# A convolution moved wholly to VectorE, a fused masked copy in a matrix inverse, and another instruction scheduler, in a two-block kernel

## The chip, the cores and the metric

The kernel runs on one core of a Trainium2 chip. The metric is the time of one execution in microseconds (us) on the device. Before the change three runs took 1193.18, 1193.24 and 1193.87 us, with a median of 1193.24 us.

The core has five engines with a queue each: TensorE (PE, with its weight loads PEld), VectorE (DVE), ScalarE (ACT), GpSimd (POOL) and SyncE (SP), which here issues the loads and stores. Each engine works through its own instructions in the order that was fixed when the kernel was built, and waits on semaphores for the others.

## What is computed

Two transformer blocks on 512 tokens of width 1024, in fp32. Cut to what matters here:

```python
# block 1: grouped attention (8 query heads, 2 key heads, 256 context keys) beside a conformer convolution
u = rms_norm(h, norm_w) * (1 + scale) + shift        # shift, scale, gate from c @ w_mod
p = u @ w_in                                         # q, k, v, gates za, glu a|g, gates zc
u2 = a * sigmoid(g)                                  # 512 tokens x 512 channels
y = depthwise_conv(u2, conv_w) + conv_b              # width 31, centred
conv = (silu(layer_norm(y)) @ w_pw + b_pw) * silu(zc)
h = h + gate * (concat(attention * silu(za), conv) @ w_out)

# block 2: rwkv7 time mix (12 heads of 64, delta rule) beside attention to 256 memory tokens, then a feed-forward
slab = token_shift((rms_norm(h) @ rw_in), mu)        # r, k, v, decay, rates, gate
for t in range(512):                                 # per head, state S is 64 x 64
    S = S * w_t + (S @ a_t) b_t^T + v_t k_t^T
    y_t = S @ r_t
x = x + concat(mix, memory_attention) @ w_out
x = x + square(relu(rms_norm(x) @ w_ff1)) @ w_ff2
```

## The kernel before

Features lie on the 128 partitions and tokens along the free axis, so a tile is mostly 128x512. Every fp32 product of the large projections is made of three matmuls (`mm3`, line 181): weights and activations are split into a high and a low part (`wh`, `wl` and a pair of `hg`, `U` or `A` tiles), and hi·hi, hi·lo and lo·hi are added in PSUM. A projection (`proj`, line 189) of one 128-column slab is 8 such triples, 24 matmuls. The high part of a weight is an ACT copy, the low part a DVE subtraction (`wl<-wr,wh`); SP loads the raw weights (`wr`) two at a time, so a load waits until the DVE subtraction has released a buffer.

**Block 1** (`block1`, line 345). The start loads `w_mod` (24 loads of 512 KB, ten buffers `modw`) and `w_start` (8 loads, two buffers `wr`), makes shift, scale and gate, normalises x to the pairs `U`, and accumulates six projections at once. `glu` turns three pairs of them into the convolution's inputs `up[0..2]` (tiles `hg`); a fourth comes after the projections `pa` and `pg`. Then follow q (four token groups in the PSUM tiles `s`), the context norm (tiles `tA`, `modw`), k and v (six token tiles), eight gate projections (`zgate`, each 24 matmuls, a tanh on ACT and one DVE operation `hg<-tA,pj`), rope and the head norms (tiles `xb`, `kn`, `nr`), the first two heads' queries (`xa<-pt,xa` on DVE), their scores (`s<-kst,xa`), and the attention, with the convolution's layer norm and pointwise product put between its heads.

The convolution has 4 channel tiles of 31 taps. The middle tap with the bias is an ACT operation that initialises `y`; the 30 others (120 in all) are spread over three engines by hand-written tables. Tiles 0 and 1 (60 taps): ACT multiplies into a tile `cv` and POOL adds (`conv_pool`; `tick` releases one tap per so many matmuls, `PACE`). Tile 2 and half of tile 3 (45 taps): one DVE `scalar_tensor_tensor` each (`conv_vec`, counts `CVQ` and `CVZ`), written into the program between the q groups and after each gate. The other 15 taps of tile 3: two POOL operations each (`conv_self`).

**Block 2** (`block2`, line 1292). Six pairs of heads. Each pair has three projections (r, k, v), a preparation (`prep`), and two groups of four 128x128 units. `gen_abc` (line 945) inverts each group's triangular matrices in 16 steps: matmuls into the PSUM tile `i`, evictions on ACT and DVE into the f16 tiles `f`. Early in it DVE makes three masked tiles `Dm`, `DT` and `P1`; then three more masked copies of `Lh`, called `OT`, are made by three POOL multiplications of 128x512, and later `IX` (identity minus X) by one more. `gen_chain` (line 1104) carries the state over the chunks (`sb`, `st`, `y`). The steps of all generators are merged by a table of due times, with the projections cut into eight pieces each (`PIECES`), and the program is written in that order. After the last pair the feed-forward runs over `w_ff1` and `w_ff2` until the end.

The build's scheduler takes the program as written and orders each engine's queue; its default is used before the change.

Of the kernel before, what the change touches and what calls it, by code (L numbers as in the profile page):

```python
# [13 lines left out]
F16 = mybir.dt.float16  # L14
# [11 lines left out]
KT = 8  # L26
# [309 lines left out]
PACE = 6  # L336
CVZ = (2, 1, 2, 0, 3, 4, 3, 3)
CVQ = (8, 9, 9, 8)
CTX = (0, 2)
CONV = (0, 0, 0, 0, 0, 0, 0, 0)  # L340
CSELF = (30, 0, 0, 1, 0, 1, 0, 0)
# [3 lines left out]
def block1(k, I, st, h1d):  # L345
# [130 lines left out]
    todo = [[w for w in range(31) if w != 15] for _ in range(4)]  # L476

    def tap(i):
        w = todo[i].pop(0)
        o0, o1 = max(0, 15 - w), min(S, S + 15 - w)  # L480
        return o0, o1, up[i][:, o0 + w - 15:o1 + w - 15], k.cw[:, i * 31 + w:i * 31 + w + 1]

    def conv_init(i):
        y = ys[i] = k.t("hg")
        A.activation(y, up[i], AF.Identity, scale=k.cw[:, i * 31 + 15:i * 31 + 16], bias=k.vec("conv_b", i))

    def conv_pool():
        r = yield
        for i in (0, 1):
            conv_init(i)  # L490
            while todo[i]:
                o0, o1, u, w = tap(i)
                p = k.t("cv")
# [8 lines left out]
    cp = conv_pool()
    pace = [0]

    def tick(r, n=1):
        pace[0] += n
        while pace[0] >= PACE:
            pace[0] -= PACE
            cp.send(r)

    def conv_self(i, n):
        if ys[i] is None:
            y = ys[i] = k.t("hg")
            G.tensor_scalar(out=y, in0=up[i], scalar1=k.cw[:, i * 31 + 15:i * 31 + 16], scalar2=k.vec("conv_b", i), op0=ALU.mult, op1=ALU.add)
        for _ in range(min(n, len(todo[i]))):
            o0, o1, u, w = tap(i)
            p = k.t("cv")
            G.tensor_scalar(out=p[:, o0:o1], in0=u, scalar1=w, scalar2=None, op0=ALU.mult)
            G.tensor_tensor(out=ys[i][:, o0:o1], in0=ys[i][:, o0:o1], in1=p[:, o0:o1], op=ALU.add)

    def conv_vec(i, n):
        if ys[i] is None:
            conv_init(i)
        for _ in range(min(n, len(todo[i]))):
            o0, o1, u, w = tap(i)
            V.scalar_tensor_tensor(out=ys[i][:, o0:o1], in0=u, scalar=w, in1=ys[i][:, o0:o1], op0=ALU.mult, op1=ALU.add)

    def conv_drain():
        while todo[0] or todo[1]:
            cp.send(None)  # L530
        conv_vec(3, 31)
        assert not any(todo)
# [10 lines left out]
    next(cp)  # L543
    pa, pg = k.t("pj"), k.t("pv")
    proj(k, pa, W1.next(), us, tick=tick)
    proj(k, pg, W1.next(), us, tick=tick)
    glu(pa, pg)

    q_ps = [k.t("s", [2, S]), k.t("s", [2, S])]
    for g in range(4):  # L550
        wh, wl = W1.next()
        for kk in range(2):
            j = 2 * g + kk
            c = slice(kk * S, (kk + 1) * S)
            for t in range(4):
# [5 lines left out]
                tick(T.matmul(ps, ul[:, tt], wh[:, c], start=False, stop=j == KT - 1), 3)  # L561
        conv_vec(2, CVQ[g])
# [15 lines left out]
    for t in (2, 3, 4, 5, 0, 1):  # L578
        ps = k.t("pt", [256])
        for j in range(KT):  # L580
# [7 lines left out]
            tick(T.matmul(ps, ul[:, tt], wh[:, c], start=False, stop=j == KT - 1), 1.5)  # L588
# [1035 lines left out]
```

## Time and profile before

| | |
|---|---|
| median of three runs | 1193.24 us |
| the profiled execution | 1195.04 us |
| its span, first to last instruction | 1193.2 us |
| TensorE busy | 1096.6 us (92%) |
| VectorE busy | 750.1 us (63%) |
| ScalarE busy | 573.7 us (48%) |
| GpSimd busy | 266.3 us (22%) |
| granted TensorE clock, mean | 0.967 |
| chain that ended last, by engine | PE 72%, DVE 17%, ACT 5%, POOL 3% |

The span has four stretches: the start to about 75 us, the rest of block 1 to about 390 us, the time mix of block 2 to about 850 us, and the feed-forward to the end. The matmuls of this core are pipelined, so busy times of TensorE overlap and a busy TensorE is not one at its peak. The granted clock is the share of full TensorE speed that the chip allowed in a stretch; its two levels are 1.2 and 2.4 GHz.

### The profile page before, as it was taken

The numbers are of one execution on the slowest core, as the hardware profiler recorded it, in microseconds if no ns is written. First come the engines' busy times: TensorE is split into PE (matmuls) and PEld (weight loads), VectorE is DVE, ScalarE is ACT, GpSimd is POOL, SyncE is SP. The second block draws the span as 40 slices with busy tenths as digits, with TensorE's granted clock in tenths as the row PEclk, the third lists the DMA queues.
The fourth block names the chain that finished last, engine by engine and source line by source line (L and its number), as shares of the span: only waits on it lengthen the run. The fifth ranks groups of instructions, "written<-read, shape, count | busy, mean of one in ns | idle before, by whom it ended". The sixth has DMA issues, their size and how long they took to land.

```text
span 1193.2 us, 16090 instructions
## 1 busy us (share of the span) xinstructions
PE 1096.6 (92%) x6268; PEld 842.1 (71%) x6268; DVE 750.1 (63%) x1161; ACT 573.7 (48%) x1047; POOL 266.3 (22%) x360
## 2 busy tenths in 40 slices
PE   7997776799999888999999988999999999999998
PEld 3665664565677766666667766776888888888887
DVE  3348999756545469888887688856544334334332
ACT  4346456567843436545464566556534224223220
POOL 0018558780000223334242234100000000000000
PEclk7999887899999989999999999999999999999999
DMA  8752111100123411101011211221232323232332
GB/s 289 251 199 71 36 46 61 53 19 7 48 84 137 123 52 36 37 19 37 19 36 37 62 50 62 72 71 54 88 106 89 105 90 104 90 102 93 99 113 88
DMA packets 30604, 96.47 MB, mean 81 GB/s; under 512 B 3392, under 2 KB 4160, under 8 KB 30528
## 3 DMA queue, kind: packets, MB, share of 16 engines
q1 hardware_dynamic: 30528, 95.45, 24.4%
q8 instruction: 49, 0.80, 0.3%
q14 instruction: 27, 0.22, 0.1%
HBM read 91.24 MB, written 4.19 MB: 80 GB/s over the span
## 4 chain that ended last, share of the span: by engine, by line
PE 72%; DVE 17%; ACT 5%; POOL 3%; issue 2%; DMA 1%; SPq 0%; DVEq 0%; ACTq 0%; POOLq 0%
PE pf L57 29%; PE pj L57 19%; PE i L57 6%; PE pt L57 6%; PE s L57 5%; DVE f L57 5%; PE pv L57 4%; DVE hg L57 3%; PE y L57 2%; POOL nr L57 2%; DVE wl L57 2%; DVE tA L57 1%; DVE p L57 1%; ACT p L57 1%; DVE nr L57 1%
## 5 line engine op out<-in xcount | busy, mean ns | idle before, releaser
L57 ACT ACTIVATE wh<-wr 128x1024 fp32r<-128x1024 f32 (+1 forms) x132 | 137.4, 1042 | 155.0 <-PE pf L57 76.4
L57 DVE TENSOR_TENSOR wl<-wr,wh 128x1024 fp32r<-128x1024 f32 (+1 forms) x132 | 162.3, 1230 | 20.6 <-PE pt L57 7.6
L57 PE MATMUL pj<-hg,wh 128*128 128x512 f32 x448 | 156.3, 417 | 3.2 <-ACT r L57 1.8
L57 PE MATMUL pf<-A,wh 128*128 128x512 f32 x512 | 157.8, 389 | 0.0
L57 POOL TENSOR_TENSOR hg<-hg,cv 128x497 f32<-128x497 f32 (+14 forms) x75 | 112.7, 1503 | 124.3 <-ACT cv L57 116.7
L57 ACT ACTIVATE f<-i 128x512 f16<-128x512 f32 (+1 forms) x132 | 73.2, 598 | 105.1 <-PE i L57 104.9
L57 PEld LDWEIGHTS pf<-A,wh 128*128 128x128 f32 x512 | 95.9, 188 | 19.9
L57 PE MATMUL pf<-A,wl 128*128 128x512 f32 x256 | 99.6, 389 | 0.0
L57 PEld LDWEIGHTS pj<-hg,wh 128*128 128x128 f32 x448 | 81.5, 192 | 19.9 <-ACT r L57 2.0
L57 DVE TENSOR_TENSOR x<-x,pf 128x512 f32<-128x512 f32 (+1 forms) x33 | 22.1, 671 | 113.9 <-PE pf L57 113.9
L57 PE MATMUL i<-f 128*128 128x128 f16 x816 | 69.7, 224 | 24.0 <-DVE f L57 23.6
L57 PE MATMUL pj<-hg,wl 128*128 128x512 f32 x224 | 90.0, 402 | 1.5 <-DVE wl L57 1.5
L57 PEld LDWEIGHTS <-f 128*128 128x128 f16 x864 | 56.7, 100 | 48.5 <-DVE f L57 24.9
L57 PE MATMUL pf<-ff,wh 128*128 128x512 f32 (+1 forms) x272 | 79.7, 377 | 0.0
L57 PE MATMUL pf<-hg,wh 128*128 128x512 f32 x256 | 78.8, 389 | 0.0
L57 DVE SCALAR_TENSOR_TENSOR fr<-pf,r 128x512 f32<-128x512 f32 x32 | 22.1, 691 | 85.4 <-PE pf L57 82.1
L57 ACT ACTIVATE fr<-fr 128x512 f32<-128x512 f32 x32 | 20.2, 632 | 100.2 <-DVE fr L57 100.2
L57 POOL TENSOR_TENSOR f<-f,c 128x512 f16<-128x512 f16 x36 | 48.0, 1361 | 74.1 <-ACT f L57 74.1
L57 PE MATMUL pj<-U,wh 128*128 128x512 f32 x160 | 53.6, 408 | 10.7 <-DVE hg L57 10.7
L57 POOL TENSOR_SCALAR nr<-nr 128x8 f32<-128x8 f32 (+2 forms) x70 | 24.9, 355 | 171.2 <-DVE nr L57 129.1
L57 PEld LDWEIGHTS pf<-ff,wh 128*128 128x128 f32 x272 | 50.1, 188 | 9.5
L57 PEld LDWEIGHTS pf<-hg,wh 128*128 128x128 f32 x256 | 48.0, 188 | 10.0
(303 smaller groups left out, 2368.0 us busy)
## 6 DMA issues: line engine op xcount, KB each, us to landing
wr<-w_ff SPq DMA_DIRECT2D x64, 512.0 KB, 3.5
modw<-w_mod SPq DMA_DIRECT2D x24, 512.0 KB, 7.2
wr<-rw_in SPq DMA_DIRECT2D x20, 512.0 KB, 3.5
wr<-w_out SPq DMA_DIRECT2D x16, 512.0 KB, 3.5
wr<-w_in SPq DMA_DIRECT2D x10, 512.0 KB, 3.5
wr<-w_start SPq DMA_DIRECT2D x8, 384.0 KB, 3.7
x<-xT SPq DMA_DIRECT2D x8, 256.0 KB, 5.7
wr<-w_q SPq DMA_DIRECT2D x4, 512.0 KB, 3.7
```

Of the source, the lines that this page charges most:

```text
L57: r = f(*a, **kw)
```

## The change

There are four parts.

- **The convolution.** All 120 taps become DVE operations. The ACT initialisation and the 30 taps of a tile are written together, the taps inside a block that lowers their scheduling priority by `LATER` = 1500. Tiles 0 to 2 are written before `pa` and `pg`, tile 3 after the fourth `glu`. The tile `cv`, the tables, and the pacing are gone.
- **The inverse.** The three POOL multiplications that made `OT` become one DVE multiplication of 128x1536 f16 (tile `lv`, two buffers; Lh broadcast over three masks). `IX` moves from POOL to DVE. `f` goes from 18 to 12 buffers.
- **The scheduler.** The build is told to order the instructions with `schedule_with_timeline_sim=True`.
- **What follows for the queues.** The new scheduler moves rows on every engine, SP's queue included. At the start SP now issues rows, constants and the rope table amid the `w_mod` loads (before: behind all of them), and the last four `w_start` loads, with the two context loads among them, after the 24th `w_mod` load (before: alternating with groups of four). POOL keeps memsets, casts and the small `nr` chains.

```diff
 LN_AFTER = (4, 4.5, 5, 5.5, 6.5, 7, 7.5, 7.5, 7.5, 8)
 MODW = 10
-PACE = 6
-CVZ = (2, 1, 2, 0, 3, 4, 3, 3)
-CVQ = (8, 9, 9, 8)
+LATER = 1500
 CTX = (0, 2)
-CONV = (0, 0, 0, 0, 0, 0, 0, 0)
-CSELF = (30, 0, 0, 1, 0, 1, 0, 0)
...
-    def conv_pool():
...
-                t = A.activation(p[:, o0:o1], u, AF.Copy, scale=w)
...
-                G.tensor_tensor(out=ys[i][:, o0:o1], in0=ys[i][:, o0:o1], in1=p[:, o0:o1], op=ALU.add)
...
+    def conv(i):
+        u, cw = up[i], lambda w: k.cw[:, i * 31 + w:i * 31 + w + 1]
         y = ys[i] = k.t("hg")
+        A.activation(y, u, AF.Identity, scale=cw(15), bias=k.vec("conv_b", i))
+        with k.tc.high_priority(offset=-LATER):
+            for w in range(31):
+                if w != 15:
+                    o0, o1 = max(0, 15 - w), min(S, S + 15 - w)
+                    V.scalar_tensor_tensor(out=y[:, o0:o1], in0=u[:, o0 + w - 15:o1 + w - 15], scalar=cw(w), in1=y[:, o0:o1],
+                                           op0=ALU.mult, op1=ALU.add)
...
-    next(cp)
+    for i in range(3):
+        conv(i)
     pa, pg = k.t("pj"), k.t("pv")
-    proj(k, pa, W1.next(), us, tick=tick)
-    proj(k, pg, W1.next(), us, tick=tick)
+    proj(k, pa, W1.next(), us)
+    proj(k, pg, W1.next(), us)
     glu(pa, pg)
+    conv(3)
...
-    OT = []
-    for j in range(1, 4):
-        o = k.t("f", [4, P], F16)
-        G.tensor_tensor(out=o, in0=Lh, in1=mk(j), op=ALU.mult)
-        OT.append(o)
+    OT = k.t("lv", [3, 4, P], F16)
+    V.tensor_tensor(out=OT, in0=Lh.rearrange("p (o u) x -> p o u x", o=1).to_broadcast([P, 3, 4, P]),
+                    in1=k.m16[:, 1:4].rearrange("p (j o) x -> p j o x", o=1).to_broadcast([P, 3, 4, P]), op=ALU.mult)
...
-    G.tensor_tensor(out=IX, in0=k.id16x4, in1=X, op=ALU.subtract)
+    V.tensor_tensor(out=IX, in0=k.id16x4, in1=X, op=ALU.subtract)
...
-    k.open(P2, "p2b", dict(lw=1, wa=1, r1=1, AR=2, BK=2, vs=2, UX=2, MT=1, E=3, R4=2, Vs=2, UV=3, W=2, QG=2, sb=2, st=2, f=18))
+    k.open(P2, "p2b", dict(lw=1, wa=1, r1=1, AR=2, BK=2, vs=2, UX=2, MT=1, E=3, R4=2, Vs=2, UV=3, W=2, QG=2, sb=2, st=2, f=12, lv=2))
...
-    with tile.TileContext(nc) as tc:
+    with tile.TileContext(nc, schedule_with_timeline_sim=True) as tc:
```

Three places in the engines' orders, first before and then after the change.

**VectorE, up to the first heads' queries** (`xa<-pt,xa`); `wl` is the low part of a gate's weight, `hg<-tA,pj` a gate's last operation, `kst` the assembled keys. Before:

```order
L57 TENSOR_TENSOR c1_83<-nr_1522,nr_1523 128x44
L57 TENSOR_SCALAR c1_83<-c1_83 128x32 x2
L57 TENSOR_TENSOR wl_1738<-wr_1736,wh_1737 128x1024
L57 TENSOR_TENSOR kst_1603<-pt_1612,kst_1603 64x256
L57 TENSOR_TENSOR kst_1603<-pt_1605,kst_1603 64x512
L57 SCALAR_TENSOR_TENSOR hg_1693<-tA_1691,pj_1648 128x512
L57 TENSOR_TENSOR kst_1604<-pt_1617,kst_1604 64x512
L57 TENSOR_TENSOR kst_1604<-pt_1624,kst_1604 64x256
L57 TENSOR_TENSOR xa_1636<-pt_1630,xa_1635 128x512
L57 TENSOR_TENSOR xa_1645<-pt_1639,xa_1644 128x512
L57 TENSOR_REDUCE c1_83<-s_1699 128x1
```

After:

```order
L57 TENSOR_SCALAR c1_83<-c1_83 128x32 x2
L57 TENSOR_TENSOR wl_1707<-wr_1705,wh_1706 128x1024
L57 SCALAR_TENSOR_TENSOR hg_1666<-tA_1664,pj_1633 128x512
L57 TENSOR_TENSOR kst_1517<-pt_1526,kst_1517 64x256
L57 TENSOR_TENSOR kst_1517<-pt_1519,kst_1517 64x512
L57 TENSOR_TENSOR kst_1518<-pt_1531,kst_1518 64x512
L57 TENSOR_TENSOR kst_1518<-pt_1538,kst_1518 64x256
L57 TENSOR_TENSOR wl_2444<-wr_2442,wh_2443 128x1024
L57 SCALAR_TENSOR_TENSOR hg_1737<-tA_1735,pj_1704 128x512
L57 TENSOR_TENSOR xa_1550<-pt_1544,xa_1549 128x512
L57 TENSOR_TENSOR xa_1559<-pt_1553,xa_1558 128x512
```

Before, six of the eight gates' last operations stand ahead of the first `xa`, and the seventh and eighth behind it. After, all eight stand ahead of it, as do all 120 taps.

**VectorE, the start of one inverse** (third pair, first group): the four `f` rows are the difference L, then `Dm`, `DT` and `P1`; the last `f` row is the eviction of the next product. Before:

```order
L57 TENSOR_TENSOR f_4764<-i_4758,f_4763 128x512
L57 TENSOR_TENSOR f_4767<-UX_4722,c2_3149 128x512
L57 TENSOR_TENSOR f_4768<-f_4763,c2_3149 128x512
L57 TENSOR_TENSOR f_4771<-f_4767,c2_3149 128x512
L57 SCALAR_TENSOR_TENSOR rk_4778<-z_4776,g_58,rk_4778 128x511
L57 TENSOR_TENSOR wl_4783<-wr_4781,wh_4782 128x1024
L57 TENSOR_TENSOR f_4796<-i_4791,c2_3149 128x512
```

After:

```order
L57 TENSOR_TENSOR f_4598<-i_4592,f_4597 128x512
L57 TENSOR_TENSOR f_4601<-UX_4556,c2_2999 128x512
L57 TENSOR_TENSOR f_4602<-f_4597,c2_2999 128x512
L57 TENSOR_TENSOR lv_4666<-f_4597,c2_2999 128x1536
L57 TENSOR_SCALAR st_4576<-y_4568,s8_3570 128x128
L57 TENSOR_TENSOR x_3825<-x_3825,bon_3325 128x512
L57 TENSOR_TENSOR f_4605<-f_4601,c2_2999 128x512
L57 TENSOR_TENSOR f_4630<-i_4625,c2_2999 128x512
```

The new `lv` row stands between `DT` and `P1`, with two operations of other work behind it; the projections' rows `rk` and `wl` that stood behind `P1` are gone from this place.

**TensorE, projections beside the inverse in block 2**; `pj<-hg,wh` and `pj<-hg,wl` are a projection's matmuls, `i<-f` the inverse's, `s` and `y` those of the scores and the state. Before:

```order
L57 MATMUL pj<-p,g 128x512
L57 MATMUL y<-g,sb 128x128
L57 MATMUL s<-AR,BK 128x128 x8
L57 MATMUL pj<-hg,wh 128x512 x2
L57 MATMUL pj<-hg,wl 128x512
L57 MATMUL pj<-hg,wh 128x512 x2
L57 MATMUL pj<-hg,wl 128x512
L57 MATMUL y<-E,UV 64x128 x2
L57 MATMUL y<-QG,st 128x128
L57 LDWEIGHTS f
L57 MATMUL i<-f 128x128
L57 LDWEIGHTS f
```

After:

```order
L57 MATMUL i_3471<-f_3438,lv_3401 128x128
L57 MATMUL pj_3751<-hg_2693,wh_3558 128x512
L57 MATMUL pj_3751<-hg_2694,wh_3558 128x512
L57 MATMUL pj_3751<-hg_2693,wl_3559 128x512
L57 MATMUL pj_3751<-hg_2734,wh_3558 128x512
L57 MATMUL pj_3751<-hg_2735,wh_3558 128x512
L57 MATMUL pj_3751<-hg_2734,wl_3559 128x512
L57 MATMUL pj_3751<-hg_2776,wh_3558 128x512
L57 MATMUL pj_3751<-hg_2777,wh_3558 128x512
L57 MATMUL pj_3751<-hg_2776,wl_3559 128x512
```

Before, the projections stand in pieces of 1 to 10 matmuls between steps of the inverse and the chain. After, many stand in one run: that of `pj_3751`, whose first nine rows are shown, has all its 24 matmuls together. In return several groups of the inverse (about five of the twelve) have no projection between their steps.

## Rows read from the trace of the kernel before

**Rows 1.** The page's part 1: busy us of each engine, share of the span, instructions.

```profile
PE 1096.6 (92%) x6268; PEld 842.1 (71%) x6268; DVE 750.1 (63%) x1161; ACT 573.7 (48%) x1047; POOL 266.3 (22%) x360
```

**Rows 2.** The windows: busy us (count) of each engine by stretch, granted clock, DMA.

```profile
core 0: us, PE busy (x) PEld busy (x) DVE busy (x) ACT busy (x) POOL busy (x), PEclk, DMA share, GB/s
75.00:225.00 150.00, 110.17 (x501) 88.55 (x500) 134.26 (x182) 87.71 (x154) 97.05 (x64) 0.84 0.19 58
180.00:210.00 30.00, 17.52 (x62) 13.49 (x61) 29.71 (x41) 19.87 (x34) 25.90 (x17) 0.78 0.18 53
225.00:245.00 20.00, 17.91 (x88) 14.14 (x88) 14.72 (x24) 11.55 (x22) 19.77 (x14) 1.00 0.08 27
450.00:700.00 250.00, 231.70 (x1905) 174.53 (x1906) 210.59 (x365) 137.27 (x317) 83.24 (x147) 0.99 0.11 35
850.00:1193.00 343.00, 339.61 (x1521) 281.98 (x1519) 135.53 (x158) 101.73 (x125) 0.00 (x0) 1.00 0.30 97
```

**Rows 3.** TensorE's waits from 105 to 245 us: us in total, times, longest.

```profile
PE pj L57 <- DVE tA L57: 10.7, 1, 10.7
PE pj L57 <- DVE hg L57: 10.7, 3, 9.8
```

**Rows 4.** The timeline from 111 to 125 us: start us, us, engine, operation.

```profile
114.12 6.48 POOL L57 TENSOR_TENSOR hg<-hg,cv 128x510 f32<-128x510 f32 x4 [1.02 <-ACT cv L57]
117.76 1.73 DVE L57 SCALAR_TENSOR_TENSOR hg<-hg,c 128x506 f32<-128x506 f32 x1
119.41 1.47 DVE L57 TENSOR_TENSOR tA<-tA 128x256 f32<-128x256 f32 x1
120.81 0.73 DVE L57 SCALAR_TENSOR_TENSOR hg<-hg,c 128x507 f32<-128x507 f32 x1
121.46 0.41 DVE L57 TENSOR_TENSOR tA<-tA 128x256 f32<-128x256 f32 x1
```

**Rows 5.** The chain of waits from 482 to 645 us: its shares by engine and tile.

```profile
by line: PE pj L57 21.8%; DVE f L57 20.1%; PE i L57 17.9%; PE y L57 9.3%; PE s L57 4.0%; DVE p L57 3.7%; POOL nr L57 3.4%; ACT f L57 2.9%; DVE BK L57 2.9%; DVE wl L57 2.5%; issue 2.2%; DVE UV L57 1.8%; DVE z L57 1.7%; DVE rk L57 1.2%; DVE s
```

**Rows 6.** The timeline from 536 to 550 us: one group's inverse begins.

```profile
536.21 4.03 POOL L57 TENSOR_TENSOR f<-f,c 128x512 f16<-128x512 f16 x3 [2.95 <-ACT f L57]
537.52 0.62 PE L57 MATMUL pj<-hg,wh 128*128 128x512 f32 x2
537.85 2.67 DVE L57 TENSOR_TENSOR f<-f,c 128x512 f16<-128x512 f16 x2
537.99 0.40 PE L57 MATMUL pj<-hg,wl 128*128 128x512 f32 x1
539.28 0.62 PE L57 MATMUL i<-f 128*128 128x128 f16 x8 [0.54 <-DVE f L57]
```

**Rows 7.** The timeline at 740 us: `DT` and `P1` of a late group.

```profile
740.45 0.76 DVE L57 TENSOR_TENSOR f<-f,c 128x512 f16<-128x512 f16 x2
```

**Rows 8.** Groups by line, whole span: count, busy us, mean ns, idle before, releaser.

```profile
L57 POOL TENSOR_TENSOR hg<-hg,cv 128x497 f32<-128x497 f32 (+14 forms) x75 | 112.7, 1503 | 124.3 <-ACT cv L57 116.7 <-DVE c L57 3.9
L57 ACT ACTIVATE cv<-hg,c 128x497 f32<-128x497 f32 (+14 forms) x60 | 41.8, 710 | 14.4 <-POOL hg L57 14.2
```

**Rows 9.** The same view: VectorE from 77 to 245 us.

```profile
L57 DVE SCALAR_TENSOR_TENSOR hg<-hg,c 128x497 f32<-128x497 f32 (+14 forms) x45 | 50.3, 1118 | 1.3 <-ACT hg L57 1.1
L57 DVE TENSOR_TENSOR wl<-wr,wh 128x1024 fp32r<-128x1024 f32 x17 | 24.4, 1435 | 7.0 <-PE pv L57 4.2 <-PE pj L57 1.6 <-PE pt L57 1.1
L57 DVE TENSOR_TENSOR tA<-tA 128x256 f32<-128x256 f32 x7 | 6.1, 871 | 0.0
```

**Rows 10.** The same view: VectorE from 450 to 700 us.

```profile
L57 DVE TENSOR_TENSOR f<-i,c 128x512 f16<-128x512 f32 x27 | 18.3, 679 | 1.7 <-PE i L57 1.6
L57 DVE TENSOR_TENSOR wl<-wr,wh 128x1024 fp32r<-128x1024 f32 x15 | 18.2, 1214 | 0.5 <-PE pj L57 0.4
```

**Rows 11.** What SyncE's DMA queue waits for from 0 to 80 us.

```profile
SPq L57 <- DVE wl L57: 42.0, 8, 8.5
```

**Rows 12.** The page's part 6: DMA issues, KB each, median us from issue to landing.

```profile
wr<-w_start SPq DMA_DIRECT2D x8, 384.0 KB, 3.7
```

More of the change, by code (lines that the diff above doesn't have):

```diff
@@ L474, in block1 @@
     ys = [None] * 4
[L476 to L483, printed above, removed]
-        y = ys[i] = k.t("hg")
-        A.activation(y, up[i], AF.Identity, scale=k.cw[:, i * 31 + 15:i * 31 + 16], bias=k.vec("conv_b", i))
-    def conv_pool():
[L488 to L493, printed above, removed]
-                t = A.activation(p[:, o0:o1], u, AF.Copy, scale=w)
-                if r is not None:
-                    k.after(t, r)
-                G.tensor_tensor(out=ys[i][:, o0:o1], in0=ys[i][:, o0:o1], in1=p[:, o0:o1], op=ALU.add)
-                r = yield
-        while True:
-            yield
@@ L502, in block1 @@
[L502 to L532, printed above, removed]
+    def conv(i):
+        u, cw = up[i], lambda w: k.cw[:, i * 31 + w:i * 31 + w + 1]
+        y = ys[i] = k.t("hg")
+        A.activation(y, u, AF.Identity, scale=cw(15), bias=k.vec("conv_b", i))
[5 more added lines that the diff above has]
+                                           op0=ALU.mult, op1=ALU.add)
@@ L560, in block1 @@
                 T.matmul(ps, uh[:, tt], wl[:, c], start=False, stop=False)
-                tick(T.matmul(ps, ul[:, tt], wh[:, c], start=False, stop=j == KT - 1), 3)
-        conv_vec(2, CVQ[g])
+                T.matmul(ps, ul[:, tt], wh[:, c], start=False, stop=j == KT - 1)
         if g == CTX[0]:
@@ L587, in block1 @@
             T.matmul(ps, uh[:, tt], wl[:, c], start=False, stop=False)
-            tick(T.matmul(ps, ul[:, tt], wh[:, c], start=False, stop=j == KT - 1), 1.5)
+            T.matmul(ps, ul[:, tt], wh[:, c], start=False, stop=j == KT - 1)
         kv = k.t("kvs", [256])
@@ L596, in zgate @@
         ps = k.t(tag)
-        proj(k, ps, W1.next(), us, tick=tick)
+        proj(k, ps, W1.next(), us)
         t = k.t("tA")
@@ L664, in zgates @@
             gz.append(zgate(zt[i] if i < 4 else "pj"))
-            conv_vec(3, CVZ[i])
     for i in range(4):
@@ L812, in block1 @@
             zgates(ZG[3 + i])
-            if i == int(LN_AFTER[0]):
-                conv_drain()
             for _ in range(LN_AFTER.count(i)):
                 next(ln, None)
-            conv_vec(3, CONV[i])
-            conv_self(3, CSELF[i])
             if half == 1 and pr < 3:
@@ L1047, in gen_abc @@
         ps = k.t("i")
-        units(ps, OT[j], X, True, True)
+        units(ps, OT[:, j], X, True, True)
         Y = k.t("f", [4, P], F16)
@@ L1506, in emit @@
         p1 = ExitStack()
-        k.open(p1, "p1", dict(c1=1, U=16, tA=4, kvs=6, cv=2))
+        k.open(p1, "p1", dict(c1=1, U=16, tA=4, kvs=6))
         k.open(p1, "p1m", dict(pj=1), PSUM)
```

## The prediction

> **What bounds the kernel now.** I read the page first, then the windows, the waits of TensorE, and last the timelines of the two places that the change touches. TensorE is busy for 92% of the span [rows 1], but evenly so only at the end: in the feed-forward from 850 us it is busy for 339.6 of 343 us with GpSimd at 0 [rows 2]. That stretch is bound by TensorE, holds no edited instruction, and I cost it at 0.
>
> From 75 to 225 us the bound is VectorE. TensorE is busy for 110.2 of 150 us at a granted clock of 0.84, VectorE for 134.3, and in 180 to 210 us VectorE for 29.7 of 30 while TensorE has 17.5 [rows 2]. TensorE's long waits from 105 to 245 us end on VectorE: 10.7 us once for the context norm's `tA`, 10.7 us in three for `hg` [rows 3]. What VectorE does there is slowed by GpSimd: while GpSimd adds its taps from 114.12 to 120.60, a VectorE tap takes 1.73 us and a 128x256 product 1.47; in the next rows, beside no GpSimd operation, they take 0.73 and 0.41, and the product starts 0.65 us after the tap [rows 4]. So a tap in a row of operations costs 0.65 us alone.
>
> In 450 to 700 us VectorE is busy for 210.6 of 250 us, TensorE for 231.7 at clock 0.99 [rows 2]. The chain there alternates: `PE pj` 21.8%, `DVE f` 20.1%, `PE i` 17.9% [rows 5]. The timeline of one group shows the same slowing: GpSimd makes the three `OT` in 4.03 us, and in that time VectorE's `DT` and `P1` take 2.67 us for two, where a late group without GpSimd needs 0.76 [rows 7]; TensorE waits 0.54 us for `DT` [rows 6].
>
> **The change, part by part.** *The convolution, 75 to 245 us.* Removed: 75 GpSimd additions of 1503 ns and 60 ScalarE products of 710 ns [rows 8]; neither engine is full there, so their own time is worth nothing. Added: 75 taps on VectorE, 75 x 0.65 = 49 us. Gained back: VectorE without GpSimd beside it. The 45 taps that it has now take 1118 ns on average, against 0.73: 17.4 us. The 17 `wl` take 1435 against 1214 [rows 9, 10]: 3.8 us. The 7 products `tA` take 871 against 410 [rows 4, 9]: 3.2 us. That is 24 us from three groups. Some forty smaller groups of the same view, each against the shortest duration of its own shape, give an estimated 26 more, so 50 in all. VectorE's work stays as it is, to within 1 us. But the two gates that now stand ahead of the first `xa` move two `wl` and two `hg` there, 2 x (1.21 + 0.68) = 3.8 us (0.68 as for 512 columns from PSUM [rows 10]). VectorE is idle for 15.7 of the 150 us [rows 2]; taps of tiles 0 to 2 need only the start's sums, so they can fill most of it. I take two thirds, 10.5. The first `xa` then comes 10.5 - 3.8 = 7 us earlier. Bounds: all idle time filled gives 12 us earlier; only the three groups' relief gives 26 - 7 = 19 us later.
>
> Behind the first `xa`, in 225 to 245 us, TensorE is busy for 17.9 of 20 us [rows 2], and two of the eight gates stand there now. One gate is 24 matmuls; from the start of two at 537.52 to the third at 537.99 an interval is 0.235 us [rows 6], so a gate is 5.6 us and two are 11. The scores that remain have their own chain with ScalarE and VectorE, so I count 8 of the 11; bounds 0 and 11. Sum for this stretch: -15 us, from +19 to -23. The attention behind it loses GpSimd's and ScalarE's last taps, which hide behind TensorE: 0.
>
> *The start.* SP's queue waits 42.0 us, in 8 times, for VectorE's `wl` to free a `wr` buffer; the longest wait is 8.5 us [rows 11]. In the new order no `w_mod` load stands behind the last four `w_start` loads, so these waits no longer hold `w_mod` back; those four loads in turn stand behind all 24 `w_mod` and the two context loads. A `w_start` load lands 3.7 us after its issue [rows 12]; two pairs that are issued only when they are needed cost 7 us. The longest wait won back is 8 us. I take -2, since the loads alternate less but the buffers are the same: from -8 to +7.
>
> *The inverse, 12 groups.* `DT` and `P1` take 2.67 us for two beside GpSimd [rows 6] and 0.76 in a late group without it [rows 7]. So `DT`, on the chain, ends 0.95 us earlier; 11 groups had it contended, 10 us. `P1` and `IX` follow in 0.41 us or less each, off the chain as long as no eviction waits behind them. GpSimd's `nr` chains no longer queue behind its taps and copies, which I count as nothing gained. The new `lv` is three times as long as an `f<-f,c`: at the f16 rate 0.41 + 2 x 0.27 = 0.95 us, at fp32 rates (1214 ns for 1024, 679 for 512 [rows 10], so 0.535 per 512) 1.75. I take 0.95, for `f<-f,c` is its nearest kin [rows 7] and 0.27 is half of 0.535. It fills the gap from `DT`'s end to the next eviction on VectorE, in which TensorE and ScalarE make the next products. So it costs nothing while that gap is over 0.95 + 0.41 us; without any gap it costs 12 x 1.36 = 16 us, and 26 at the slow price. The Trainium skill (VectorE: DVE Perf Modes, "The perf-mode tier table") gives a product of two 16-bit SBUF tensors two elements a cycle, and its mode needs a step of one in each; the broadcasts here keep that step in the innermost dimension, so by the page the estimate is 0.96 us. No row of this trace shows a broadcast f16 operand.
>
> The same order moves projections into runs of 24. A run is 5.6 us in which a finished eviction has to wait for TensorE. The 18 projections of heads are 101 us of TensorE, and `PE pj` holds 21.8% of the chain already [rows 5], so part of the cost of a run is paid now. I charge 2 us net: -10 + 2 = -8 for block 2, from -23 (the two copies' whole 1.91 us, 12 times) to +37 (below). With `f` at 12 instead of 18 buffers, `OT` has its own two, so no new wait for a buffer is counted.
>
> Sum against the profiled execution of 1195.0 us: -15 - 2 - 8 = -25, or 1170. The runs' median lies 1.8 us lower, so **1168 us**.
>
> **The rivals.** *Projections in clumps* (slower). In three pairs, 163 us, the chain holds 35.5 us of `PE pj` [rows 5], while nine projections need 9 x 5.6 = 50.8: at least 30% hide now between steps that wait for VectorE. If runs of 24 put all into the chain, 18 projections lose 30 us. About five groups have then no filler at all; where TensorE idled, in 180 to 210 us, the granted clock was 0.78 against 0.99 in the busy block 2 [rows 2]. At 0.78 the inverse's 4.9 us of matmul per group (17.9% of 163 us over six groups) grow by 1.3, 7 us for five groups. If lv takes the slow price off the gap, 10 more. Together -10 + 30 + 7 + 10 = +37, and with the -17 of start and block 1 the profiled time is 1215. It decides from +17 on, where 27 of these 47 us are lost. I price it midway between 1195 and 1215: 1205, or 1203 for the runs. For it: `PE pj` leads the chain. Against it: TensorE's waits for `f` are short now, so runs stand where the inverse is waiting anyway. The Trainium skill's Perfetto Trace Analysis, "Matmul Optimizations", wants matmuls in back-to-back batches since the engine's power follows its use; by that rule the runs keep the clock up, and the bare groups let it fall.
>
> *VectorE overfull.* The taps aren't really last: if they stand ahead of `wl`, norm and rope, each is 0.65 us of delay for TensorE. With only the three groups' relief, block 1 is +19 - 8 = +11, and with -2 - 8 it is 1196, or 1194 for the runs: no change. The Trainium skill's Perfetto Trace Analysis, "Optimizing Scalar/DVE Operations", advises moving work off a saturated VectorE to ScalarE or GpSimd, and warns that the two share a read port; by the advice alone the change adds its 49 us to the full engine, less 10.5 of idle time, hence 1195 + 39 = 1234. The slowing beside GpSimd speaks for the warning [rows 4].
>
> *Half the gain.* One of block 1 and block 2 gives nothing: 1178 to 1187.
>
> *The larger gain.* All idle time is filled and all four `DVE f` fall: -23 - 2 - 23 = -48, so 1147, or 1145 for the runs.
>
> **How the numbers follow.** Changes within 0.2%, 2.4 us, can't be told from none. The forecast with its own range (1156 to 1178) gets 0.40, half the gain 0.18, the larger gain 0.12: faster by over 0.2% 0.70. VectorE overfull gets 0.10, of which 0.06 falls within 0.2% and 0.04 above. Clumps get 0.20, nearly all slower by over 0.2%: 0.23 slower, 0.07 the same. For the 8 in 10 I leave out the far halves of the larger gain and of the clumps: 1146 to 1205.
>
> **What would show it.** Right: GpSimd nearly 0 after 75 us; taps at 0.73 us; the eight gates done before the first `xa`, which comes near 218 us; the gates' matmuls gone from the 20 us behind it; `f<-f,c` at 0.41, `lv` near 0.95; three pairs of block 2 in about 159 us, where they take 163 now. Wrong: TensorE still waiting over 5 us in 105 to 245 us; `lv` at 1.75; three pairs in over 169 us, with `PE pj` above 25% of their chain; a start that ends after 80 us.

## The result, and the profile after the change

The change made the kernel **slower**: 1230.82 us, median of four runs (1229.69 to 1232.99), against 1193.21 us for the kernel before beside it. The ratio is 1.0323, with a 95% interval of 1.0300 to 1.0346. The forecast was 1168 us with a range up to 1205. Its sign was wrong and the time lies outside the range.

The page's part 1 of the kernel after, to set against [rows 1]. TensorE does the same 6268 matmuls, but is busy 25 us longer; GpSimd's work is down from 266 to 64 us, as intended.

```profile
PE 1121.7 (91%) x6268; PEld 864.5 (70%) x6268; DVE 727.1 (59%) x1260; ACT 537.1 (44%) x987; POOL 63.7 (5%) x222
```

The windows of the kernel after, with the columns and the stretches of [rows 2]:

```profile
75.00:225.00 150.00, 120.06 (x543) 96.39 (x542) 133.71 (x251) 51.41 (x96) 0.00 (x0) 0.85 0.19 60
225.00:245.00 20.00, 14.18 (x68) 10.17 (x66) 12.02 (x22) 10.49 (x20) 0.00 (x0) 0.83 0.09 27
450.00:700.00 250.00, 223.08 (x1716) 172.60 (x1715) 175.90 (x341) 122.95 (x284) 31.70 (x106) 0.91 0.09 28
```

Two things stand out. In 75 to 225 us VectorE is idle for 16.3 of 150 us, as long as before (15.7): the taps filled none of that time. In 450 to 700 us VectorE lost its load (175.9 for 210.6), yet TensorE issues 1716 matmuls where it issued 1905, and the granted clock fell from 0.99 to 0.91. Part of both falls is work that now comes behind 700 us.

The sizes, though, are what the prediction took. The groups by line of VectorE over the whole span of the kernel after (count, busy us, mean ns), to set against [rows 4, 7, 9]:

```profile
L57 DVE SCALAR_TENSOR_TENSOR hg<-hg,c 128x500 f32<-128x500 f32 (+14 forms) x120 | 82.4, 732 | 0.5 <-ACT hg L57 0.5
L57 DVE TENSOR_TENSOR lv<-f,c 128x1536 f16<-128x1536 f16 x12 | 11.4, 948 | 0.0
L57 DVE TENSOR_TENSOR f<-f,c 128x512 f16<-128x512 f16 x24 | 9.9, 414 | 0.0
```

So these operations are no dearer than priced; the loss must lie in the order, which the experiments test. Rows of the timeline of the kernel after in the context norm (start us, us, engine, operation; idle time before it and what ended it; some rows in between are left out) show one place:

```profile
138.55 0.73 DVE L57 SCALAR_TENSOR_TENSOR hg<-hg,c 128x506 f32<-128x506 f32 x1
139.21 1.42 DVE L57 TENSOR_TENSOR tA<-modw 128x256 f32<-128x256 f32 x4
139.65 2.08 ACT L57 ACTIVATE modw<-tA,c 128x256 fp32r<-128x256 f32 x4 [3.00 <-DVE tA L57]
140.31 0.38 PE L57 MATMUL pt<-wh,modw 128*128 128x256 f32 x1 [3.76 <-ACT modw L57]
140.55 2.70 DVE L57 SCALAR_TENSOR_TENSOR hg<-hg,c 128x506 f32<-128x506 f32 x4
143.17 1.04 DVE L57 TENSOR_SCALAR tA<-tA,c 128x256 f32<-128x256 f32 x3
144.14 0.73 DVE L57 SCALAR_TENSOR_TENSOR hg<-hg,c 128x507 f32<-128x507 f32 x1
145.12 2.04 DVE L57 SCALAR_TENSOR_TENSOR hg<-hg,c 128x506 f32<-128x506 f32 x3
147.09 1.08 DVE L57 TENSOR_TENSOR modw<-tA,modw 128x256 fp32r<-128x256 f32 x3
147.55 0.50 PEld L57 LDWEIGHTS pt<-wh,modw 128*128 128x128 f32 x2 [6.71 <-DVE modw L57]
```

Eight taps stand among the norm's steps between 140.55 and 147.09 us, and TensorE waits for `modw` behind them. A low priority did not put the taps last: in the trace all 120 start before the first `xa`.

**Where the time went.** The table cuts each execution at five landmarks of its timeline: VectorE's first `xa<-pt,xa`, TensorE's last attention matmul `pv<-xb,kvs`, VectorE's first `f<-UX,c` (block 2's first group begins), the ninth such (eight groups are done), and TensorE's last `y<-QG,st` (the last group's chain ends). The columns are the stretches between, in us, for all kernels of this study; "rest" goes to VectorE's last operation, some 3 us before the span's end. They come from one profiled execution of each kernel, the last column is the median of its runs; the two differ most for e4, whose profiled execution took 1167.6 us. The experiments follow below.

| kernel | to first `xa` | attention | to first group | eight groups | to chain's end | rest | runs |
|---|---|---|---|---|---|---|---|
| before | 224.8 | 118.6 | 94.6 | 207.2 | 155.1 | 389.8 | 1193.2 |
| **after** | 226.5 | 118.2 | 98.3 | 237.1 | 153.9 | 390.9 | 1230.8 |
| e1 after, default scheduler | 172.1 | 136.4 | 95.6 | 198.8 | 153.4 | 389.8 | 1150.9 |
| e2 before, new scheduler | 244.3 | 117.8 | 98.3 | 247.2 | 173.9 | 393.3 | 1281.3 |
| e3 before, inverse's edit | 220.6 | 121.1 | 94.5 | 195.3 | 153.8 | 389.8 | 1181.1 |
| e4 before, convolution's edit | 177.7 | 136.8 | 96.0 | 205.6 | 156.7 | 389.8 | 1161.9 |
| x1 projections held | 228.3 | 118.1 | 90.4 | 223.5 | 157.1 | 391.0 | 1211.1 |
| x4 runs by hand (on e1) | 173.1 | 135.9 | 97.1 | 204.9 | 153.5 | 389.8 | 1160.5 |
| x5 taps held | 215.8 | 120.8 | 96.1 | 237.1 | 155.1 | 390.1 | 1220.0 |
| x6 = x1 + x5 | 218.8 | 121.9 | 90.6 | 223.6 | 156.4 | 390.7 | 1209.8 |
| x7 side steps held | 228.8 | 118.1 | 93.2 | 229.7 | 168.2 | 389.6 | 1230.0 |
| x8 taps in the attention | 191.3 | 136.1 | 96.7 | 241.3 | 154.4 | 390.6 | 1215.6 |
| x9 = x7 + x8 | 190.0 | 136.3 | 91.1 | 228.9 | 168.5 | 390.0 | 1212.7 |
| y1 TensorE's order of e1 | 220.2 | 143.0 | 95.0 | 218.5 | 159.5 | 389.3 | 1228.5 |
| y2 VectorE's order of e1 | 184.1 | 148.5 | 103.8 | 233.8 | 176.1 | 400.7 | 1255.0 |
| y3 ScalarE's order of e1 | 210.4 | 147.0 | 98.3 | 235.4 | 164.0 | 402.9 | 1261.4 |
| y4 = y1 + y2 | 175.9 | 144.4 | 99.0 | 200.2 | 158.4 | 390.0 | 1176.6 |
| y6 all five orders of e1 | 173.1 | 136.8 | 95.9 | 195.4 | 153.5 | 389.9 | 1151.6 |
| z1 e1 with taps early | 214.7 | 122.7 | 95.8 | 198.7 | 153.4 | 389.9 | 1177.8 |

After against before, 35 us by the trace: up to block 2's first group +5, the eight groups +30, the rest about 0.

### The profile page after: what moved, and what is told of

The parts are those of the page before. It is cut to its first block, busy times and chain, and to the rows that moved or that the text cites. A ratio compares the mean times of both kernels' runs of the same rounds, so it can differ in the third digit from the quotient of the medians.

```text
span 1227.8 us, 15912 instructions
## 1 busy us (share of the span) xinstructions
PE 1121.7 (91%) x6268; PEld 864.5 (70%) x6268; DVE 727.1 (59%) x1260; ACT 537.1 (44%) x987; POOL 63.7 (5%) x222
## 4 chain that ended last, share of the span: by engine, by line
PE 42%; DVE 5%; ACT 2%; POOL 2%; issue 1%; DMA 0%; POOLq 0%; DVEq 0%; ACTq 0%
PE pf L57 28%; PE pj L57 8%; PE i L57 4%; PE y L57 2%; POOL nr L57 1%; DVE f L57 1%; PE s L57 1%; DVE p L57 1%; DVE wl L57 0%; ACT AR L57 0%; ACT f L57 0%; DMA wr<-w_out 0%; DVE x L57 0%; ACT p L57 0%; DVE c L57 0%
## 5 line engine op out<-in xcount | busy, mean ns | idle before, releaser
L57 DVE TENSOR_TENSOR wl<-wr,wh 128x1024 fp32r<-128x1024 f32 (+1 forms) x132 | 158.5, 1201 | 26.6 <-PE pt L57 10.5
L57 PE MATMUL pj<-hg,wh 128*128 128x512 f32 x448 | 148.7, 412 | 1.4 <-ACT r L57 0.7
L57 PEld LDWEIGHTS pj<-hg,wh 128*128 128x128 f32 x448 | 84.2, 194 | 24.0 <-issue 2.8
L57 DVE SCALAR_TENSOR_TENSOR hg<-hg,c 128x500 f32<-128x500 f32 (+14 forms) x120 | 82.4, 732 | 0.5 <-ACT hg L57 0.5
L57 PEld LDWEIGHTS <-f 128*128 128x128 f16 x720 | 52.2, 109 | 37.9 <-issue 20.7
L57 PE MATMUL i<-f 128*128 128x128 f16 x672 | 62.0, 241 | 16.6 <-DVE f L57 15.4
L57 PE MATMUL pj<-U,wh 128*128 128x512 f32 x160 | 58.9, 449 | 11.8 <-DVE hg L57 11.8
L57 PEld LDWEIGHTS pf<-A,wl 128*128 128x128 f32 x256 | 48.1, 188 | 10.0
L57 DVE TENSOR_REDUCE c<-s 128x1 f32<-128x768 f32 (+1 forms) x36 | 34.6, 982 | 28.9 <-PE s L57 28.9
L57 PE MATMUL pf<-ff,wl 128*128 128x512 f32 (+1 forms) x136 | 50.1, 376 | 0.0
```

What stands on the lines that cost most here:

```text
L57: r = f(*a, **kw)
```

## The experiments

### The parts apart: e1 to e4

"S" in the expectations is the theory that the scheduler's order loses the time. e1 is the changed kernel with the default scheduler; e2 is the kernel before with the new one. e3 and e4 put the inverse's and the convolution's part of the diff alone on the kernel before.

```diff
-    with tile.TileContext(nc, schedule_with_timeline_sim=True) as tc:
+    with tile.TileContext(nc) as tc:
```

> The changed kernel with the default scheduler; convolution and inverse as changed. Theory S (the scheduler's order loses the time, in block 2 above all): the loss is gone and the relief of VectorE from GpSimd remains, 1170 to 1190 us, the first eight groups of the inverse in about 200 us against 207 before and 237 changed. Rival C (the taps and copies that moved to VectorE lose it): 1215 us or more.

> The kernel before with the new scheduler alone; convolution and inverse as before, GpSimd included. Theory S: slower than before, 1215 to 1250 us, with bare groups and runs of projections in block 2. Rival C: within 5 us of 1193.

> The kernel before with the inverse's masked copies on VectorE as changed, nothing else. Theory S: 1180 to 1190 us, since DT ends about 1 us earlier in each group and lv at 0.95 us hides. Rival C: 1200 us or more, lv standing in the chain.

> The kernel before with the convolution as changed (all taps on VectorE at low priority), inverse and scheduler as before. Theory S: 1178 to 1193 us, block 1 up to 15 us shorter. Rival C: 1200 us or more, block 1 longer.

Ratios to the kernel before: e1 0.9647 [0.9612, 0.9681], e2 1.0731 [1.0685, 1.0776], e3 0.9902 [0.9868, 0.9936], e4 0.9742 [0.9698, 0.9786]. The two edits of the code gain 12 and 31 us apart, 42 together. The scheduler costs 88 us on the kernel before and 80 on the edited one. So the whole loss is the scheduler's, and e1, at **1150.89 us, beats both kernels**. Theory S has the signs right in all four, but e1 and e4 are faster and e2 is slower than the ranges that it gave.

The windows of e1, columns as above; its first `xa` comes at 172 us, so the second row is its stretch up to there:

```profile
75.00:225.00 150.00, 140.09 (x786) 111.16 (x786) 141.80 (x280) 83.39 (x157) 0.00 (x0) 1.00 0.22 66
75.00:172.00 97.00, 90.37 (x487) 75.84 (x488) 93.30 (x195) 48.70 (x91) 0.00 (x0) 1.00 0.28 85
225.00:245.00 20.00, 17.99 (x108) 10.84 (x109) 18.73 (x32) 12.61 (x25) 0.00 (x0) 1.00 0.08 27
450.00:700.00 250.00, 237.82 (x1941) 179.80 (x1940) 199.98 (x401) 143.89 (x334) 42.25 (x140) 0.97 0.13 41
```

Up to its first `xa` TensorE now does 487 matmuls in 97 us at a granted clock of 1.00, where the kernel before did 501 in 150 us at 0.84 [rows 2] and the kernel after 543 at 0.85. (The 786 of the first row reach into the attention.) TensorE's waits in e1 from 105 to 245 us, against the 10.7 and 10.7 of [rows 3] (the two longest):

```profile
PE pj L57 <- DVE hg L57: 3.6, 2, 3.1
PE s L57 <- ACT p L57: 1.5, 2, 1.2
```

In e1 and e4 61 taps start before the first `xa` and 59 behind it, the last at 262 and 268 us. That is where e4 gains more than the prediction's 15: the first `xa` comes 47 us earlier and the attention, which now carries half the taps, takes only 18 longer. z1, below, tests this.

### Projections and taps: x1, x4, x5, x6

x1 orders the first matmul of each projection piece behind the preceding step of an inverse, so that the new scheduler can't draw pieces together:

```diff
+        if self.cur == "abc":
+            self.step = r
+        elif self.cur == "pj" and self.fresh:
+            self.fresh = False
+            if self.step is not None:
+                self.after(r, self.step)
```

x4 is e1 with whole projections: the runs of 24 without the new scheduler.

```diff
-PIECES = 8
-PJ = (-23.6, 0.59)
+PIECES = 1
+PJ = (-23.6, 4.72)
```

x5 orders the first tap of tiles 1 to 3 behind the context norm's last `modw` operation; x6 is x1 and x5 together.

```diff
-    for i in range(3):
-        conv(i)
+    conv(0)
...
-    conv(3)
...
+    for i in range(1, 4):
+        conv(i, last[0])
```

> The changed kernel, new scheduler, with one order added in block 2: the first matmul of each projection piece goes behind the last matmul of the inverse step that is written before it, so projections stay in pieces of 3 or 6. Theory R (runs of projections and bare groups lose block 2's time): the first eight groups take 200 to 208 us instead of 237, the total 1190 to 1205 us. Rival D (it is the order of VectorE and ScalarE in block 2, such as the state's copies that TensorE waits for): 1220 us or more.

> The default scheduler with convolution and inverse as changed (1151 us), but the projections written in one piece of 24 matmuls instead of eight, at the same mean spacing. Theory R: block 2 loses part of what the new scheduler lost, 8 to 30 us, total 1160 to 1180. Rival D: within 4 us of 1151.

> The changed kernel, new scheduler, with the 90 taps of tiles 1 to 3 ordered behind the last VectorE operation of the context norm. Theory T (taps between the steps of the context norm hold k, v and the gates back in block 1): k and v are done by 145 us instead of 166, total 1200 to 1215. Rival E (block 1 is late for another reason, taps fill idle time): within 6 us of 1231, or later.

> Both orders added to the changed kernel. If theories R and T hold and add up, 1160 to 1185 us, near the default scheduler's 1151; if the new order loses its time in many places, 1195 us or more.

Ratios to the kernel before: x1 1.0150 [1.0124, 1.0176], x4 0.9738 [0.9703, 0.9774], x5 1.0237 [1.0194, 1.0280], x6 1.0138 [1.0100, 1.0176]. Holding the projections wins 20 us back, 14 of them in the eight groups; longer runs alone, in the default order, cost 10. The default scheduler still splits most of x4's projections (three runs of 24 and five of 16 up to the end of the eighth group), so x4 prices runs only as far as they form. So the clumps are real, but holding them wins back only 14 of the 38 us that the eight groups lose against e1. Holding the taps behind the norm wins 11 us: the last `kvs`, the end of k and v, comes at 136 us for 167, but 113 of the 120 taps still start before the first `xa`. The two don't add: x6 is where x1 is. x1 and x5 fall between their two theories.

### Side steps, and taps in the attention: x7, x8, x9

x7 orders the first TensorE, VectorE and ScalarE instruction of every step of `project`, `gen_chain`, `prep` and `finish` behind the engine's last inverse instruction. x8 writes the taps of tiles 2 and 3 behind the first `xa`; x9 is both.

```diff
+        if self.cur == "abc":
+            self.step[e] = r
+        elif self.cur == "held" and e not in self.fresh:
+            self.fresh.add(e)
+            if e in self.step:
+                self.after(r, self.step[e])
```

```diff
-    for i in range(3):
+    for i in range(2):
         conv(i)
...
-    conv(3)
...
+    for i in range(2, 4):
+        conv(i, k.latest[V])
```

> The changed kernel, new scheduler; in block 2 the first TensorE, VectorE and ScalarE instruction of each projection piece, chain step, preparation and finish goes behind the last one of the inverse step written before it. Holding the projections alone gave 1211 us. Theory Q (the new order puts chain and preparation work ahead of the inverse's evictions in VectorE's and ScalarE's queues, where it waits for TensorE): the first eight groups fall from 223 us to 195 to 210, the total to 1180 to 1198. Rival (the rest of the loss lies inside the steps, or in TensorE's order alone): 1205 us or more.

> The changed kernel, new scheduler, with the 60 taps of tiles 2 and 3 ordered behind the first heads' queries, as the default scheduler leaves about half of them there. Theory T2 (the new order packs all 120 taps ahead of the first queries, VectorE being the bound there and half idle in the attention): first queries at 180 to 200 us instead of 226, the attention's end 15 to 30 us earlier, total 1200 to 1216. Rival E (taps fill idle time; block 1 is late for another reason): 1222 us or more.

> Both of the last two together. If both theories hold, their gains add: 1155 to 1180 us, near the default scheduler's 1151; if they lie on the same path or fall, 1190 us or more.

Ratios to the kernel before: x7 1.0272 [1.0225, 1.0318], x8 1.0154 [1.0125, 1.0184], x9 1.0138 [1.0084, 1.0193]. x7 is a miss: what its groups gain (7 us) the stretch behind them loses (14), so holding these steps behind the inverse is no remedy; whether single ones among them cost time is not shown. x8 holds: the first `xa` comes 35 us earlier and the attention takes 18 more, 15 us net in the runs.

### Which engine's queue: y1 to y6

These keep the new scheduler but fix the order of the named engines to that of e1, each instruction ordered behind the one ahead of it in a table. y1 does so for TensorE, y2 for VectorE, y3 for ScalarE, y4 for TensorE and VectorE, y6 for all five.

```diff
+def as_ordered(k):
+    for row in ORDERS:
+        prev = None
+        for n in row.split():
+            r = k.made.get("I-" + n)
...
+            if prev is not None:
+                k.tc.add_manual_dep(r.ins, prev.ins.name, SCHED, reason="order")
+            prev = r
```

> The change, with TensorE's queue alone put into the order that the default scheduler gives the same program (e1, 1151); the other engines' orders are left to the new scheduler. Theory TensorE (the loss lies in its clumped projections and in gates ahead of the attention): 1150 to 1175, and the groups of block 2 return to about 25 to 27 us each. Theory VectorE (the loss lies in taps, low parts and lv that stand ahead of evictions): 1215 to 1235, little changed. Theory shared (either order alone leaves the other engine out of step): in between, 1180 to 1215.

> The change, with VectorE's queue alone put into the default scheduler's order; TensorE's stays clumped. Theory VectorE: 1150 to 1175. Theory TensorE: 1200 to 1230, no better than the run that put the taps of two tiles into the attention (1216). Theory shared: 1180 to 1215, most of it gained in block 1, where the taps stand behind the queries again, while the groups of block 2 stay near 30 us.

> The change, with ScalarE's queue alone put into the default scheduler's order. All theories expect little: 1215 to 1235, since ScalarE is busy for 44% of the span. Below 1200 would say that its evictions and weight copies stand in the wrong order, which no theory named.

> The change, with the queues of both TensorE and VectorE in the default scheduler's order. If these two hold the whole loss, it comes within 10 us of e1's 1151. If the rest (ScalarE's, GpSimd's and the loads' order) holds a part, it stays above 1165 by that part.

> The change, with the queues of TensorE, VectorE, ScalarE, GpSimd and SyncE all in the default scheduler's order: a control. If the flag acts through the order of the queues alone, this comes within 0.5% of e1's 1151 and the 24 us that y4 (1177) still lacks go with the remaining queues; if it stays near 1177, the flag changes something else (buffers, semaphores) that no queue's order shows.

Ratios to the kernel before: y1 1.0279 [1.0244, 1.0315], y2 1.0500 [1.0420, 1.0581], y3 1.0551 [1.0513, 1.0588], y4 0.9847 [0.9798, 0.9895], y6 0.9644 [0.9612, 0.9676]. No theory had the single queues right: y1 is where theory VectorE put it, but y2 and y3 are slower than every range given. One queue of e1's among four others gains nothing (y1) or loses 24 and 31 us (y2, y3). Two that fit each other win 54 of the 80 us, and all five win the whole. y6 shows that the flag costs its time through the queues' order and nothing else (1151.6 us for e1's 1150.9). By the traces each named queue has e1's order row by row (operation and tile, without buffer numbers). In y4 GpSimd's 222 rows have it too, though nothing ordered them, so the 25 us from y4 to y6 lie with ScalarE's queue (651 of 987 rows in e1's places) and SyncE's (190 of 212 loads and stores).

The stretch of the first eight groups shows both forms of the loss. In the windows of the kernel after, of e1, of y1, of y4 and of the kernel before (one fence each, columns as above):

```profile
443.00:680.00 237.00, 210.39 (x1584) 160.81 (x1583) 166.30 (x320) 113.61 (x259) 29.35 (x98) 0.91 0.09 28
```

```profile
404.00:603.00 199.00, 193.20 (x1582) 144.26 (x1582) 165.58 (x322) 111.27 (x258) 32.73 (x98) 0.98 0.11 33
```

```profile
458.00:677.00 219.00, 197.41 (x1582) 147.81 (x1581) 166.00 (x321) 112.94 (x258) 25.94 (x98) 0.96 0.09 30
```

```profile
419.00:620.00 201.00, 192.22 (x1583) 143.94 (x1582) 166.24 (x322) 112.82 (x259) 32.43 (x98) 0.99 0.10 33
```

```profile
438.00:645.00 207.00, 192.27 (x1580) 143.50 (x1579) 177.36 (x306) 110.29 (x258) 73.10 (x130) 0.99 0.10 32
```

The work is the same to four matmuls. After the change TensorE is idle for 26.6 us, in e1 for 5.8; that is 21 of the 38 us. The other 17 are the same matmuls at a lower granted clock: 210.4 us busy at 0.91 against 193.2 at 0.98. Against the kernel before the 30 us are 12 of idle time (26.6 for 14.7) and 18 of slower matmuls (210.4 for 192.3, clock 0.91 for 0.99). What the idle time waits for, in the waits of TensorE, kernel after from 443 to 680 us:

```profile
PE i L57 <- DVE f L57: 14.9, 16, 2.7
PE y L57 <- ACT x L57: 5.1, 5, 1.4
PE i L57 <- DVE UX L57: 3.3, 5, 1.7
PE y L57 <- DVE st L57: 2.1, 3, 1.2
```

The same of y1 from 458 to 677 us:

```profile
PE y L57 <- DVE st L57: 8.7, 9, 1.7
PE i L57 <- ACT f L57: 4.7, 5, 1.5
PE i L57 <- DVE UX L57: 3.7, 2, 1.9
```

And the wait for `f` on VectorE in e1 from 404 to 603 us and in the kernel before from 438 to 645 us (one fence each):

```profile
PE i L57 <- DVE f L57: 2.2, 4, 0.7
```

```profile
PE i L57 <- DVE f L57: 13.9, 21, 1.9
```

So this wait is not new: the code's edits take it from 13.9 to 2.2 us, and the new order brings it back. With TensorE's order mended (y1) it is nearly gone (1.0 us), and in its place TensorE waits for the chain's `st`, which VectorE's unmended queue has late. With both mended (y4) the stretch is back to 200 us.

Where both forms lie, the windows of the kernel after show. Its TensorE issues no projection `pj<-hg` between 574 and 607 us; the stretch before that is full of them:

```profile
545.00:574.00 29.00, 28.59 (x191) 21.86 (x190) 17.99 (x33) 15.62 (x32) 6.82 (x21) 1.00 0.12 37
574.00:607.50 33.50, 27.88 (x233) 21.22 (x232) 26.08 (x53) 14.28 (x38) 1.95 (x10) 0.80 0.06 17
588.00:599.00 11.00, 9.45 (x67) 7.43 (x67) 7.75 (x17) 5.06 (x13) 0.00 (x0) 0.53 0.00 0
```

Two other stretches are without projections, 501 to 545 and 638 to 670 us; their granted clock is 0.84 each. The three hold 22 of the 26.6 us of idle time. A piece of the timeline within, between 588 and 599 us, shows TensorE waiting for VectorE and ScalarE in turn, with no row of `pj` that could fill a gap. Here the waits are short; what is lost is the clock, 0.53, close to the lower of its two levels:

```profile
589.35 0.70 PE L57 MATMUL y<-E,UV 128*64 128x128 f32 x4 [0.34 <-DVE st L57]
591.07 1.03 PE L57 MATMUL i<-f 128*128 128x128 f16 x8 [0.29 <-DVE f L57]
593.02 0.47 PE L57 MATMUL y<-g,sb 128*128 128x128 f32 x1 [0.91 <-ACT x L57]
```

### Taps early, without the new scheduler: z1

z1 is e1 with the taps' priority lowered by 300 instead of 1500, nothing else.

```diff
-LATER = 1500
+LATER = 300
```

> e1 (default scheduler) with LATER at 300 in place of 1500: 114 taps then stand ahead of the first heads' queries on VectorE, where e1 has 52. If taps ahead of the queries are dear by themselves, at 0.65 us each less the idle time that they fill, the first xa comes 25 to 40 us later than in e1 and the attention gives part of it back: 1155 to 1175. If VectorE fills only idle time with them, within 5 us of 1151.

The ratio is 0.9859 [0.9829, 0.9889], 1177.8 us: 27 us slower than e1, a little more than expected. In the trace all 120 taps start before the first `xa` (61 in e1), which comes 43 us later; the attention gives 14 back, and block 2 is as in e1. The longest waits of TensorE in z1, 105 to 245 us, name the price:

```profile
PE pv L57 <- DVE wl L57: 37.4, 1, 37.4
PE pt L57 <- DVE wl L57: 3.2, 2, 2.8
```

One low part `wl` stands behind a run of taps, and TensorE waits 37 us for it. In the timeline of z1 the run begins with 42 taps, one right behind the other; the `wl` comes at 172.02 us:

```profile
129.55 27.52 DVE L57 SCALAR_TENSOR_TENSOR hg<-hg,c 128x510 f32<-128x510 f32 x42
172.02 1.21 DVE L57 TENSOR_TENSOR wl<-wr,wh 128x1024 fp32r<-128x1024 f32 x1
```

z1 says what the place of the taps is worth, without the new scheduler: up to the attention's end it takes 337 us, e1 309, the kernel after 345. So taps ahead of the first queries alone cost 29 us there, of the 36 that the kernel after loses against e1; x8, which puts half of them behind under the new scheduler, wins 17 back. It also leaves little of the convolution's edit: z1 is 3 us faster than e3, which has the inverse's edit alone.

## Why the prediction was wrong

**The sizes held.** Taps alone are 0.65 us apart (3 in 2.04 us, 4 in 2.70), `wl` is back at 1214 ns from 77 to 245 us, `DT` and its kin take 414 ns, and `lv` 948 ns against the 0.95 taken. The estimate for `lv` that the prediction worked out from the Trainium skill's table (VectorE: DVE Perf Modes, "The perf-mode tier table") is 0.96 us. The trace agrees with its 948 ns, broadcasts and all. The code's gain in block 2 was taken as 10 us and is 10.1 from the first group to the chain's end (362.3 us before, 352.2 in e1; with the inverse's edit alone, e3, it is 13.2). The feed-forward, taken as 0, is +1.

**The first failed step: "runs of 24 ... I charge 2 us net".** The new order costs block 2 not 2 but 39 us against the same code in the default order (391.0 against 352.2). The sign that I had named, three pairs in over 169 us, appeared: the third to the eighth group take 175 us, where they took 161 by the same landmarks. The bound for it, 30 + 7 + 10 = 47 us in the rival of the clumps, had the size. That is partly luck, for its parts came out otherwise. `lv` at the slow price, 10, did not happen. Longer runs of projections cost 10 us by themselves (x4) and holding them wins 14 in the groups (x1). The rest needs the order of TensorE and VectorE against each other (y1 and y4). The groups left bare, with their fallen clock, were the right place, and the term that was mis-sized most: I gave the clock 7 us, and 17 of the first eight groups' 38 us are matmuls at a lower clock, with 21 of idle time beside it. Projections alone don't mend it: with the pieces held (x1) TensorE still idles for 20.7 us there, at a clock of 0.95.

**The second: "they can fill most of it. I take two thirds, 10.5".** The taps filled nothing; VectorE's idle time in 75 to 225 us is 16.3 where it was 15.7. With all 120 taps ahead of the first `xa`, that came 1.7 us later instead of 7 earlier. The 8 us for the gates that left the stretch behind it didn't come either: the attention takes 118.2 us for 118.6, and in 225 to 245 us the granted clock is 0.83 where it was 1.00. Block 1 with the start is +5 up to the first group instead of -17. The step that failed is the path: I counted VectorE's idle time as a sum, but what counts is what TensorE waits for behind the taps, here the norm's `modw` and the gates' `hg`, in z1, where the taps' place alone costs 29 us, a gate's `wl`. The signal I had named, TensorE still waiting over 5 us there, did appear; the waits of the kernel after from 105 to 245 us, against [rows 3]:

```profile
PE pj L57 <- DVE hg L57: 11.8, 3, 6.5
PE pt L57 <- DVE modw L57: 6.5, 1, 6.5
PE pt L57 <- ACT modw L57: 4.0, 2, 3.8
```

**The start**, -2, is +0.6 by TensorE's last `s<-U` matmul, among the last of the accumulated projections (75.6 us for 75.0). SyncE waits for `wl` as often and as long as in [rows 11]; its longest wait has doubled, from 8.5 to 17.9 us (from 0 to 80 us):

```profile
SPq L57 <- DVE wl L57: 41.0, 8, 17.9
```

**The rivals were priced as if they excluded each other.** "VectorE overfull" and "Projections in clumps" both follow from one thing, the new order, and came together: block 1 at +11 and block 2 at +37, with -2 for the start, give 1195 + 46 = 1241, or 1239 for the runs; measured is 1231. The range stopped at 1205 because no case held both.

**The edit that I mistrusted is the good one.** Moving the taps from GpSimd and ScalarE to VectorE gains 31 us alone (e4), twice the 15 that I gave it, since in the default order half of them lie in the attention: with all taps early (z1) little of it is left. The Trainium skill's Perfetto Trace Analysis, "Optimizing Scalar/DVE Operations", says that work may be moved off a saturated VectorE, and warns that it shares a read port with GpSimd. By the advice alone the prediction priced the move as a loss of 39; the taps' 1118 ns beside GpSimd [rows 9] and 732 alone fit the warning. The Trainium skill's Perfetto Trace Analysis, "Matmul Optimizations", wants matmuls back to back. The trace agrees in that the granted clock is 0.91 in the stretch with 26.6 us of gaps and 0.98 in that with 5.8; but with the 14.7 us of gaps of the kernel before, in groups that all have projections, it was 0.99.

**What stays open.** The queues' order is shown to be the whole cause (y6), TensorE's and VectorE's together two thirds of it (y4). Why the new scheduler chose that order was not tried, and the last 25 us are not split between ScalarE's and SyncE's queues. Which rows of TensorE's and VectorE's orders cost block 2 what x1 does not win back is not shown either.

## What to carry to other kernels

Price a scheduler or a queue order as a part of its own, with its own range, and time it apart from the edits that it comes with: here the edits gained 42 us and the order lost 80. Where moved work comes to stand can be worth nearly as much as the move: with the same 120 taps all ahead of the first queries the kernel took 27 us more (z1 against e1). Check in the new order what stands *behind* each batch of filler work on the engine that TensorE waits for; a low priority isn't a place. And rivals that share a cause belong in one case, with their prices added.

## What the runs showed of the chip that I had not expected

Idle time of TensorE was paid twice: in the first eight groups 21 us of added gaps, e1 to the kernel after, came with 17 us of slower matmuls, the granted clock falling from 0.98 to 0.91. How the gaps lie matters: 14.7 us of them went with a clock of 0.99 in the kernel before, while 5.6 us in a stretch of 33.5 without projections went with 0.80 in the kernel after. In block 1 it worked the other way: with the waits gone, e1's granted clock up to the first `xa` was 1.00 where it had been 0.84, and 487 matmuls took 97 us where 501 had taken 150. And the queues are a fit of all five: e1's order on VectorE or ScalarE alone, beside the new order on the others, was 24 and 31 us slower than the new order everywhere.
